# Tags of the operand tiles in the second product of a squared-ReLU MLP

## The chip, the cores and the metric

The kernel runs on one core of a Trainium2 chip. The time is that of one execution on the device in microseconds, as the median of several runs. The profile is that of one execution, and its times are counted from the start of its span. TensorE multiplies matrices (PE; PEld is its load of weights), VectorE (DVE), ScalarE (ACT) and GpSimd (POOL) work element by element, SyncE (SP) issues nearly all of the DMAs.

## The reference

A transformer block on 1024 rows of 1024 float32 values: two token mixers (latent attention and grouped attention with axial rotation), merged by gates; then the MLP that this case is about; then an embedding added through a gate, and a last norm. Only the MLP and what follows it matter here:

```python
h2 = rmsnorm(x, g_mlp[i])
u = jax.nn.relu(jnp.einsum("bsd,df->bsf", h2, w_up[i]))     # 1024 -> 4096
x = x + jnp.einsum("bsf,fd->bsd", u * u, w_down[i])         # 4096 -> 1024
h3 = rmsnorm(x, g_ple[i])
gate = jax.nn.sigmoid(jnp.einsum("bsd,de->bse", h3, w_ple_gate[i]))
x = x + gate * jnp.einsum("bsk,kd->bsd", p[i], w_ple[i])
return rmsnorm(x, g_final)
```

## The kernel before

**Products in three passes.** A float32 operand is split in two parts: the high part is its cast to float32r (on ACT), the low part is the difference of the two (on DVE, a few on POOL). A product is three matmuls: high by high, high by low, low by high (`mm3`, line 126).

**Seven block products instead of eight.** Both MLP products are made from 2 x 2 blocks by sums and differences of blocks, with seven products. The first product (`up_pair`) takes 16 pairs of column tiles, b = 0 to 15. For each it squares the four quarters after the ReLU (`uq`), forms four sums of quarters, the tiles `us` (lines 1055 to 1060; by DVE for the last pair, by POOL otherwise), and stores these and three quarters to the DRAM array `u_d` (line 1062, 256 KB each). They are the left operands of the second product. SP issues the stores in one queue with the loads.

**The second product** goes over four chunks c = 0 to 3 of 1024 of the 4096 inner values. In each chunk the block products run in the order 1, 2, 5, 6, 3, 7, 4. A block product has four steps k; in each step one left tile `da` (from `ua`, two loads of 512 KB for each block product, line 991) and one right tile `db` (from `wd`, halves of 1 MB of `w_down`, line 985, with differences `wd` minus `wd` made by POOL in `minus`, line 1198) are split by `operand`. Each is [128, 2, 512]: the high part in the first half, the low part in the second. Twelve matmuls follow in a step: three for each of four row tiles, 48 in a block product. `put` (lines 1140 and 1142) adds the finished sum to an accumulator `acc`, by copies on ACT the first time; `acc[0]` and `acc[1]` hold the residual, loaded from `x_d` (line 1084, 2 MB each). For chunk 0, the left tiles of products 1 and 2 and the first half of `wd` are loaded ahead of the last pair (`down_first`); the other loads are issued after it in the text.

**Where the operand tiles lie.** The pool `dp` has one buffer for each tag, 4 KB per partition. The tags are given in turn, `d0` to `d9`, one for each call of `operand`, in the order a, b of step 0, a, b of step 1 and so on; there are 224 calls. A tag can be written again when the matmuls that read the tile before it are done. `dp` begins at the address at which the pool `fp` of the first product began, when that pool is closed. `fp` holds, in this order, raw weights (8 KB), `p1` (8), `st` (8), `u2` (4), `u3` (4) and then five buffers `us` of 2 KB. So `d0` to `d7` cover what comes ahead of `us`, and `d8` and `d9` lie on four of the five `us` buffers. A tile that takes such a place waits until the last reader of the old one is done, for `us` the store to DRAM.

**Order.** Engines take their instructions in the order in which the scheduler wrote them; it places an instruction by priority and by its own estimate of when operands are there, so one engine's order can interleave two block products. In the text around line 1109 nothing fixes that order.

Of the kernel before, what the change touches and what calls it, by code (L numbers as in the profile page):

```python
# [10 lines left out]
F32R = mybir.dt.float32r  # L11
# [8 lines left out]
P = 128  # L20
# [33 lines left out]
def hybrid_block_kernel(ctx: ExitStack, tc, x, p, g_mix, w_in, g_qa, w_qb, g_kva, w_kvb, g_qn, g_kn,  # L54
# [34 lines left out]
    def raw_tile(name, shape):  # L89
        return wpool.tile(shape, F32, tag="raw", name=f"raw_{name}")  # L90
# [422 lines left out]
    with tc.tile_pool(name="ap", bufs=2, reuse_waits="tile") as ap:  # L513
# [273 lines left out]
        for i in range(NK + 2):  # L787
# [3 lines left out]
            d = i - 2  # L791
# [35 lines left out]
    with tc.tile_pool(name="op", bufs=2, reuse_waits="tile") as op:  # L827
# [115 lines left out]
        for n, f in enumerate((0, 2, 1)):  # L943
            t = raw_tile(f"early{f}", [P, NK, P])
# [161 lines left out]
    na, nd, np_ = [0], [0], [0]  # L1106
    with tc.tile_pool(name="dp", bufs=1, reuse_waits="tile") as dp:
        def operand(name, raw, eng):
            t = dp.tile([P, 2, 512], F32R, tag=f"d{nd[0] % 10}", name=f"d{name}")
            nd[0] += 1  # L1110
            act.copy(t[:, 0], raw)  # L1111
            eng.tensor_tensor(t[:, 1], raw, t[:, 0].bitcast(F32), ALU.subtract)  # L1112
            return t

        def product(i, c, av, bv):
# [34 lines left out]
            for k in range(4):  # L1150
                eng = pool if c == 0 and i == 1 and k < 2 else dve
                ab.append((operand(f"a{k}_{i}_{c}", av[k // 2][:, k % 2], eng), operand(f"b{k}_{i}_{c}", bv[:, k], eng)))
                if whole:
                    continue
                for s in range(4):
                    if k == 0:
                        room(s)
                    part(s, k, k + 1)
                    if k == 3:
                        put(s)  # L1160
# [205 lines left out]
```

## Time and profile before

| | |
|---|---|
| median of 3 runs | 1686.15 us (1685.62 to 1687.7) |
| profiled execution | 1688.77 us, span 1687.0 us, mean granted clock 0.972 |
| TensorE busy | 1556.5 us, 92% of the span |
| VectorE busy | 1210.6 us, 72% |
| ScalarE busy | 816.0 us, 48% |
| GpSimd busy | 729.1 us, 43% |
| DMA | 262.56 MB, mean 156 GB/s |

The span is some 2 us shorter than the execution's own time. Busy shares are means over stages with different limits: the attention up to about 700 us, the output products, the first MLP product up to 1203 us, the second from there to 1549 us, and the gate at the end.

### The profile page before, as it was taken

How to read it: one execution, taken by the hardware profiler on the slowest of the kernel's cores; microseconds unless marked ns; L12 is line 12 of the kernel's file. 1: busy time of each engine (PE TensorE's matmuls, PEld its weight loads, DVE VectorE, ACT ScalarE, POOL GpSimd, SP SyncE). 2: the span in 40 equal slices, each digit the busy share in tenths (PEclk: the TensorE clock that was granted, in tenths of full speed). 3: DMA queues.
4: the chain of work that ended last, by engine and by line, in shares of the span. 5: the costliest groups of instructions: out<-in, count | busy, mean ns of one | idle time of the engine just before them, and what ended most of it. 6: DMA issues, size and time to landing. Idle time of an engine off the chain costs nothing.

```text
span 1687.0 us, 24112 instructions
## 1 busy us (share of the span) xinstructions
PE 1556.5 (92%) x8490; PEld 1317.4 (78%) x8490; DVE 1210.6 (72%) x1967; ACT 816.0 (48%) x1583; POOL 729.1 (43%) x463
## 2 busy tenths in 40 slices
PE   7999989998989787899996999999679999998898
PEld 7998767776767565688995888888568888876898
DVE  7277227776888878655468998999556878898753
ACT  6344327776888777533354222222145444434443
POOL 4354004645777778422153422333421322253653
PEclk9999999999999999999997999999889999999999
DMA  6024558989999999945543544444936353411232
GB/s 226 26 51 114 142 150 169 209 186 197 204 176 194 197 182 201 247 153 188 175 138 112 170 150 161 139 154 153 385 103 221 101 187 113 137 63 63 88 125 77
DMA packets 437865, 262.56 MB, mean 156 GB/s; under 512 B 284520, under 2 KB 383472, under 8 KB 437360
## 3 DMA queue, kind: packets, MB, share of 16 engines
q1 hardware_dynamic: 436464, 258.92, 58.9%
q10 hardware_dynamic: 1280, 2.10, 0.6%
q8 instruction: 67, 1.10, 0.3%
q14 instruction: 54, 0.44, 0.1%
HBM read 142.41 MB, written 49.35 MB: 114 GB/s over the span
## 4 chain that ended last, share of the span: by engine, by line
PE 50%; DMA 11%; DVE 9%; ACT 7%; issue 4%; POOL 2%; SPq 1%; ACTq 0%; POOLq 0%; DVEq 0%
PE u L126 17%; PE d L126 15%; DMA PT<-hl 7%; PE wo L126 5%; PE y L126 4%; PE pg L126 3%; ACT p L594 2%; POOL hl L602 2%; PE av L772 2%; PE gt L126 1%; DVE p L591 1%; ACT hl L600 1%; DMA wd<-in_w_down_dram 1%; DVE db L1112 1%; PE pp L126 1%
## 5 line engine op out<-in xcount | busy, mean ns | idle before, releaser
L602 POOL TENSOR_TENSOR hl<-p,hl 128x1024 f16<-128x1024 f32 x128 | 279.3, 2189 | 201.0 <-PE gt L126 83.2
L126 PE MATMUL d<-db,da 128*128 128x512 f32 x1344 | 312.2, 395 | 32.8 <-ACT db L1111 25.0
L126 PEld LDWEIGHTS d<-db,da 128*128 128x128 f32 x1344 | 255.9, 191 | 88.6 <-ACT db L1111 25.4
L126 PE MATMUL u<-H_t,wop 128*128 128x512 f32 x768 | 183.3, 394 | 5.9 <-ACT H_t L900 4.6
L126 PEld LDWEIGHTS u<-H_t,wop 128*128 128x128 f32 x768 | 145.8, 190 | 38.2 <-ACT H_t L900 5.0
L591 DVE TENSOR_SCALAR_CACHE_REDUCE p<-s 128x1024 f32<-128x1024 f32 x128 | 155.6, 1218 | 16.6 <-PE s L126 6.2
L1111 ACT CAST da<-ua 128x512 fp32r<-128x512 f32 x112 | 69.7, 623 | 182.2 <-PE d L126 140.8
L594 ACT ACTIVATE p<-p,mx 128x1024 f32<-128x1024 f32 x128 | 147.2, 1150 | 9.3 <-DVE Va L458 1.5
L126 PE MATMUL u<-H_b,wop 128*128 128x512 f32 x576 | 137.8, 393 | 7.1 <-ACT wop L815 7.1
L1112 DVE TENSOR_TENSOR da<-ua,da 128x512 fp32r<-128x512 f32 x110 | 89.4, 813 | 66.7 <-ACT da L1111 66.7
L126 PEld LDWEIGHTS u<-H_b,wop 128*128 128x128 f32 x576 | 109.1, 190 | 30.2 <-ACT wop L815 7.5
L1198 POOL TENSOR_TENSOR wd<-wd,wd 128x1024 f32<-128x1024 f32 x16 | 39.3, 2458 | 203.4 <-DVE db L1112 195.8
L601 DVE TENSOR_SCALAR_CACHE_REDUCE hl<-p 128x512 f16<-128x512 f32 x128 | 87.2, 682 | 51.7 <-DMA PT<-hl 35.6
L1112 DVE TENSOR_TENSOR db<-wd,db 128x512 fp32r<-128x512 f32 x110 | 113.5, 1032 | 1.3 <-ACT db L1111 1.3
L126 PE MATMUL s<-KT,QT 96*128 96x512 f32 x384 | 102.4, 407 | 7.2 <-DVE p L591 7.1
L126 PE MATMUL gt<-hH,lo_g 128*128 128x512 f32 x256 | 102.0, 399 | 1.8 <-DVE lo_g L105 1.8
L126 PE MATMUL gt<-hH,hi_g 128*128 128x512 f32 x256 | 101.9, 398 | 1.6 <-ACT hi_g L103 1.6
L1057 POOL TENSOR_TENSOR us<-uq 128x512 f32<-128x512 f32 x15 | 19.6, 1307 | 192.6 <-DVE uq L1053 192.6
L126 PE MATMUL gt<-hL,hi_g 128*128 128x512 f32 x256 | 100.8, 394 | 0.0
L105 DVE TENSOR_TENSOR lo_g<-raw_g,hi_g 128x1024 fp32r<-128x1024 f32 x32 | 46.1, 1440 | 69.6 <-ACT hi_g L103 69.6
L600 ACT CAST hl<-p 128x512 f16<-128x512 f32 x128 | 78.7, 616 | 26.8 <-DMA PT<-hl 24.0
L126 PEld LDWEIGHTS s<-KT,QT 96*128 96x128 f32 x384 | 69.2, 191 | 24.8 <-DVE p L591 8.2
(341 smaller groups left out, 3923.3 us busy)
## 6 DMA issues: line engine op xcount, KB each, us to landing
ua<-u_d SPq DMA_DIRECT2D x56, 512.0 KB, 3.5
raw_g<-in_w_in_dram SPq DMA_DIRECT2D x32, 512.0 KB, 4.2
raw_up<-in_w_up_dram SPq DMA_DIRECT2D x32, 512.0 KB, 4.9
u_d<-us SPq DMA_DIRECT2D x64, 256.0 KB, 2.1
wd<-in_w_down_dram SPq DMA_DIRECT2D x16, 1024.0 KB, 9.4
u_d<-uq SPq DMA_DIRECT2D x48, 256.0 KB, 2.0
gates_d<-gst SPq DMA_DIRECT2D x32, 256.0 KB, 2.6
gg<-gates_d SPq DMA_DIRECT2D x16, 512.0 KB, 3.1
```

The costliest lines, as they stand in the source:

```text
L105: eng.tensor_tensor(lo, raw, hi.bitcast(F32), ALU.subtract)
L126: return [pe.matmul(ps, a, b, start=start and i == 0, stop=stop and i == len(m) - 1) for i, (a, b) in list(enumerate(m))[first:last]]
L591: dve.tensor_scalar(e, ps, 1.0, 3e38, op0=ALU.mult, op1=ALU.min, accum_out=mx)
L594: act.activation(e, e, AF.Exp, bias=mx, scale=-1.0, accum_out=sums[:, hd, qt:qt + 1])
L600: act.copy(hl[:, 0, :CUT], e[:, :CUT])
L601: dve.tensor_scalar(hl[:, 0, CUT:], e[:, CUT:], 1.0, 0.0, op0=ALU.mult, op1=ALU.max, accum_out=top)
L602: pool.tensor_tensor(hl[:, 1], e, hl[:, 0], ALU.subtract)
L772: pe.matmul(av[:, :256], values(hd, kt), PT[(2 * g + half) % 3][:, n, kt], start=(kt + n == 0), stop=(kt + n == NS))
L1057: eng.tensor_tensor(v[1], q[:, 2], q[:, 3], ALU.add)
L1111: act.copy(t[:, 0], raw)
L1112: eng.tensor_tensor(t[:, 1], raw, t[:, 0].bitcast(F32), ALU.subtract)
L1198: pool.tensor_tensor(o[:, ks], a[:, ks], b[:, ks], ALU.subtract)
```

## The change

The tag of an operand tile is computed in another way; nothing else differs. The n-th tile took tag n mod 10. Now the tiles 0 to 23 (products 1, 2 and 5 of chunk 0) take n mod 8, and those from 24 on take (n - 16) mod 10, so that tile 24 has `d8`, tile 25 `d9` and tile 26 `d0`. The pool has the same ten tags of the same size.

```diff
         def operand(name, raw, eng):
-            t = dp.tile([P, 2, 512], F32R, tag=f"d{nd[0] % 10}", name=f"d{name}")
+            n = nd[0]
             nd[0] += 1
+
+            t = dp.tile([P, 2, 512], F32R, tag=f"d{n % 8 if n < 24 else (n - 16) % 10}", name=f"d{name}")
             act.copy(t[:, 0], raw)
             eng.tensor_tensor(t[:, 1], raw, t[:, 0].bitcast(F32), ALU.subtract)
             return t
```

## Rows read from the trace of the kernel before

**Rows 1.** Page part 2: TensorE's busy tenths in 40 slices of 42.2 us.
```profile
...
PE   7999989998989787899996999999679999998898
...
```

**Rows 2.** Chain of waits, 1190 to 1260: start, duration (us), what held the chain.
```profile
...
1224.98 6.28 DMA u_d<-us
...
1231.33 0.63 ACT db L1111
...
1232.00 28.17 PE d L126 x116
```

**Rows 3.** Waits, 1190 to 1300: engine, line, waited for; total us, times, longest.
```profile
...
PE d L126 <- ACT db L1111: 25.0, 1, 25.0
ACT da L1111 <- DMA u_d<-us: 23.4, 1, 23.4
...
```

**Rows 4.** Timeline, 1185 to 1250: start, duration, what, [idle before <- releaser].
```profile
...
1203.70 3.33 PE L126 MATMUL d<-db,da 128*128 128x512 f32 x14
...
1205.27 0.62 ACT L1111 CAST db<-wd 128x512 fp32r<-128x512 f32 x1
...
1229.32 0.62 ACT L1111 CAST da<-ua 128x512 fp32r<-128x512 f32 x1 [23.43 <-DMA u_d<-us]
...
1232.00 18.20 PE L126 MATMUL d<-db,da 128*128 128x512 f32 x72 [24.96 <-ACT db L1111]
...
```

**Rows 5.** SyncE's queue in the timeline, 1165 to 1300: start and duration of issue.
```profile
...
1198.85 0.45 SPq L991 DMA_DIRECT2D ua<-u_d  x1
1200.08 0.32 SPq L1084 DMA_DIRECT2D acc<-x_d  x1
1200.67 0.37 SPq L991 DMA_DIRECT2D ua<-u_d  x1
1204.41 5.19 SPq L985 DMA_DIRECT2D wd<-in_w_down_dram  x2
1209.66 6.54 SPq L991 DMA_DIRECT2D ua<-u_d  x1
...
1217.43 0.52 SPq L991 DMA_DIRECT2D ua<-u_d  x1
1218.05 3.11 SPq L1062 DMA_DIRECT2D u_d<-us  x3
...
1224.98 0.32 SPq L1062 DMA_DIRECT2D u_d<-us  x1
1246.02 27.26 SPq L991 DMA_DIRECT2D ua<-u_d  x6
...
```

**Rows 6.** Stretches: length, busy PE, PEld, DVE, ACT, POOL (instructions), clock, DMA share, GB/s.
```profile
...
1207.00:1232.00 25.00, 0.04 (x1) 0.00 (x1) 3.36 (x7) 1.29 (x3) 9.23 (x4) 0.59 0.92 362
1232.00:1235.00 3.00, 3.00 (x7) 2.42 (x8) 1.88 (x3) 0.99 (x2) 0.00 (x0) 0.50 0.00 0
...
1240.00:1306.00 66.00, 66.00 (x293) 54.65 (x292) 46.13 (x56) 37.90 (x64) 15.36 (x6) 1.00 0.49 167
...
```

**Rows 7.** Timeline, 1185 to 1262: operand subtractions, casts, and POOL's differences.
```profile
...
1208.36 0.69 DVE L1112 TENSOR_TENSOR da<-ua,da 128x512 fp32r<-128x512 f32 x1
1208.96 0.68 DVE L1112 TENSOR_TENSOR db<-wd,db 128x512 fp32r<-128x512 f32 x1
...
1209.78 4.63 POOL L1198 TENSOR_TENSOR wd<-wd,wd 128x1024 f32<-128x1024 f32 x2 [7.60 <-issue]
...
1249.15 2.72 POOL L1198 TENSOR_TENSOR wd<-wd 128x1024 f32<-128x1024 f32 x1
1249.54 2.88 DVE L1112 TENSOR_TENSOR db<-wd,db 128x512 fp32r<-128x512 f32 x1
...
1255.22 0.62 ACT L1111 CAST da<-ua 128x512 fp32r<-128x512 f32 x1 [1.58 <-PE d L126]
1255.75 0.62 ACT L1111 CAST db<-wd 128x512 fp32r<-128x512 f32 x1
...
```

**Rows 8.** Groups by line, 1232 to 1560, TensorE: count, busy, mean ns, idle before.
```profile
...
L126 PE MATMUL d<-db,da 128*128 128x512 f32 x1330 | 308.9, 395 | 32.8 <-ACT db L1111 25.0 <-DVE db L1112 3.1 <-DVE v_ple L167 2.7
...
```

## The prediction

> **What bounds the kernel now.** The page's busy times come first: TensorE (PE) is busy 92% of the span, so the whole span can only shorten where PE stands still. The forty slices say where that is: besides the start and the end, PE falls to 6 and 7 tenths in the 29th and 30th slice (1181 to 1265 us) [rows 1]. The chain of waits of that stretch gives the story in three pieces: a store of `us` that lands at 1224.98 + 6.28 = 1231.26 us, then the cast of a `db`, then PE, which goes on at 1232.00 [rows 2]. The list of who waited for whom sizes it: PE waited 25.0 us once for that cast, and ScalarE (ACT) waited 23.4 us once, at the cast of a `da`, for the store `u_d<-us` [rows 3]. The engines' timeline shows both ends: PE runs 14 matmuls of the first product from 1203.70 to 1207.03 and then nothing for 24.96 us. ACT's eighth operand cast is at 1205.27; the ninth and the tenth come only at 1229.32 and 1231.33 [rows 4].
>
> Why a cast waits for a store: the ninth and tenth operand tiles take the tags `d8` and `d9`, which lie where the last pair's sums `us` lay, and those still have to be copied out. SyncE's queue (SP) issues the stores behind everything that it sent before: `ua`, 2 MB of `acc`, two `wd` of 1 MB, more `ua`, and then the sums, the last one at 1224.98 [rows 5]. From 1207 to 1232 the DMA engines are 92% busy at 362 GB/s [rows 6]: this is a queue that drains at its rate, and the store is at its end. Nothing that PE needs for the next products is among what is stored.
>
> The resumption comes exactly at the end of the tenth tile's cast although 34 matmuls of the first product were still to do: PE takes its instructions in their written order, and the first uses of the second product's operands stand in it after those 14.
>
> **What the change does, part by part.**
>
> *The ninth and tenth tile move from `d8`, `d9` to `d0`, `d1`.* Their first eight tags lie below the sums. That these are free of the stores, the trace shows: the eighth cast ended at 1205.89, and ACT's one long wait for a store comes right before the ninth [rows 3, 4]. What the ninth now waits for is the end of the first product's first step (12 matmuls), which read `d0` and `d1`. PE's rate in the dense stretch is 66.00 us for 293 matmuls, 0.225 us each [rows 6]; 12 of them from 1203.70 end at 1206.4. In the steady part a cast follows PE and the second one starts 0.53 us after it and takes 0.62 us [rows 7], so both are done at about 1207.6. Removed: the 24.96 us of PE's gap.
>
> *The clock.* In the gap the granted clock falls: the mean is 0.59, and it is 0.50, the lower of the two levels (1.2 of 2.4 GHz), from 1232 to 1235, where PE started 7 matmuls in 3.00 us [rows 6]. At 0.225 us they would take 1.6: 1.4 us more go with the gap.
>
> *Data for the products that come earlier.* This is what could be late next. Products run in the order 1, 2, 5, 6, 3; at 48 matmuls, 10.8 us each, they start at 1203.7, 1214.5, 1225.3, 1236.1 and 1246.9 if nothing stalls. The queue is in order and its last 256 KB land at 1231.26, so what stands behind a load gives its landing, at 362 to 400 GB/s an estimate from [rows 5, 6]. Product 5's second `ua` (issued 1198.85) has 7168 KB behind it (2048 of `acc`, 2048 of `wd`, three `ua` of 512, the four `us` of rows 5 and two `uq` at 256 each), 7.3 MB or 18 to 20 us: it lands at about 1211 to 1213, and its cast is due after 1220. Product 6's `ua` (1200.67) has 4608 KB behind it, 12 to 13 us: 1219, due 1230. Product 3's second (1217.43) has 1280 KB, 3.5 us: 1228, due 1240. The `acc` tile that product 2 adds into was sent before the first of these and is needed from about 1224. The weights' differences were formed by GpSimd (POOL) in four operations from 1209.78 on, 2.3 us each [rows 7], so both halves of `wd` had landed by then. All are in time, with 5 us and more to spare: cost nothing.
>
> *POOL and VectorE (DVE) meet.* In the old run DVE ended its last subtraction at 1209.64 and then stood still while POOL made those four in a row, 4.63 us for each two [rows 7]. Now DVE makes product 2's low halves in just that time. Where the two meet, a DVE subtraction of 0.68 us takes 2.88 and POOL's takes 2.72 [rows 7]: they take turns. The page "SBUF — State Buffer" of the Trainium skill, section "SBUF: two separate sides", has the rule: a DVE operation with two SBUF inputs and a GpSimd operation share a port pair by an exclusive lock, and the second blocks fully; the 2.88 us agree with that; it says nothing of how much of a block PE would see. By turns of 2.73 us from 1209.8, DVE ends its second to fifth subtraction at about 1213.0, 1215.7, 1218.4 and 1221.2, and the last three, 0.6 us apart, by 1223.0. PE needs the second (step 0) at 1214.5, the fourth (step 1) at 1217.4, the sixth (step 2) 2.7 us later, the eighth after that. So it waits about 1.0 us in step 1 and 0.7 us in step 2. Bounds: 0, if POOL starts later than now, and 4 x (2.88 - 0.60) = 9.1 us, if every blocked subtraction is exposed. I take 1.7, the count by turns.
>
> *PE's written order.* If product 2's first matmuls stay behind those 14, PE waits from 1206.85 to 1207.6, some 0.8 us; if the new order puts them later, nothing. I take 0.4.
>
> *Eight tags in turn instead of ten, up to the 24th tile.* An operand can be made four steps ahead instead of five. From the release by PE to the second low half a step takes about 1.15 us of casts and 1.3 us of subtractions [rows 7], 2.5 us, against three steps of 2.7 us = 8.1 us. It costs nothing as long as that holds.
>
> *The 25th and 26th tile (product 6, step 0) take `d8`, `d9` and now meet the stores.* The casts can start at 1231.3, the low halves are there at about 1234, and PE starts product 6 at 1236.1 plus the stalls above, at about 1238. Nothing, with 4 us of slack; ACT stands still a few us before, with no eviction due.
>
> *All later tiles, in ten tags as before, are shifted by a constant.* Loads and stores of the later chunks are released by the work itself and move with it. The last product holds `d0` to `d7` instead of `d6` to `d9` and `d0` to `d3`; the tiles of the last stage that lie there wait for the last matmul by either. From 1232 to 1560 PE idles 32.8 us before operand matmuls, 25.0 of them this gap [rows 8]; the other 8 lie near the end, and a shifted order may lengthen or shorten them: 0, with 2 us to either side as bounds.
>
> **Sum.** 24.96 + 1.4 - 1.7 - 0.4 = 24.3 us less. The profiled execution took 1688.77 us with a span of 1687.0; it becomes 1664.5 with a span of 1662.7. The median of the runs, 1686.15, is 2.62 us below the profiled one, so 1661.9 us is the time forecast. Without a stall it would be 26.4 us less (1659.8), with 9.1 us of blocked subtractions and 0.8 of order 16.5 less (1669.7); the 2 us of the end on both sides give 1657.8 to 1671.7.
>
> **Rivals.**
>
> 1. *The exclusive port decides.* If PE exposes each blocked subtraction, the gain is 16.5 us: 1669.7. For it: 2.88 us rows, four POOL operations in a row. Against: PE stays fully busy from 1240 to 1306 although pairs of them occur there [rows 6, 7].
> 2. *The wait moves to product 6.* Tiles 25 and 26 wait for the very same stores. From a landing at about 1236 on, each later us is lost again. For it: the stores are last in an in-order queue; against: what follows them in that queue, six loads of `ua`, was issued from 1246.02 on [rows 5]. With the stores 10 us later, six of them are lost: 1668.
> 3. *Nothing changes.* PE would stop at 1207 for something else that comes at 1231, or the low tags would wait for the stores too. Against it are the first eight casts [rows 4]: 1686.
> 4. *Slower: four steps ahead are too few.* If making a step's operands (two casts, two subtractions, each blocked) took longer than three steps of PE, 8.1 us, PE would wait in every one of the 8 steps of products 2 and 5, and from 3.1 us a step on that exceeds the 24.3 us gained. At 11.6 us for a step's operands it would be 3.5 us a step, 28 in all, and the time 1690. Against it: fully blocked they take 1.15 + 2 x 2.88 = 6.9 us, under the point at which it begins.
>
> **How the numbers follow.** The forecast has 0.78 (its own range 1658 to 1666), rival 1 0.08, rival 2 0.06, another order of the written work in the first chunk with a stall of 5 to 10 us 0.03, no change 0.03, slower 0.02. Runs of this kernel differ by some 0.1%, so about 0.2% (3.4 us) can be told from no change. Faster 0.95, same 0.03, slower 0.02. The range 1657.5 to 1671 takes in the bounds of the unknown costs and most of rivals 1 and 2.
>
> **What would show it.** Right: no wait of ACT for `u_d<-us` before the 25th operand tile, PE dense from 1203.7 on but for 1 to 2 us near 1217 to 1222, the granted clock at 1.00 from 1207 to 1240, and the last operand matmul some 24 us earlier. Rival 1: DVE rows of 2.88 us with PE waiting for `db` of DVE line 1112. Rival 2: a PE wait behind the 25th tile's cast at 1236 or later. Wrong altogether: a PE gap of over 10 us that begins between 1207 and 1250.

## The result, and the profile after

The changed kernel took 1674.38 us (median of 4 runs, 1672.75 to 1678.28), the kernel before 1686.93 us (4 runs, 1685.62 to 1688.97): a ratio of 0.9930 with an interval of 0.9911 to 0.9949. By the medians that is 12.6 us less, by the interval 8.6 to 15.0, where 24.3 were forecast. The direction was right, the size was half, and the time lies outside the range of 1657.5 to 1671.

The page shows that the dip at the start of the second product is still there. The 29th slice has 9 and the 30th 6 tenths now, of 41.8 us each:

```profile
...
PE   7999989998989888899996999999969999998898
...
```

The chain of waits of that stretch has the same head as before [rows 2]: a store of `us`, then casts, then PE. Columns: start, duration, what held the chain.

```profile
...
1218.57 4.36 DMA u_d<-us
...
1222.94 0.63 ACT da L1113
...
1224.88 0.61 DVE db L1114
...
1225.54 34.63 PE d L126 x144
```

The first row names the store that was issued last. By the program the cast waits for an earlier one, `us1` of the last pair, the first of that pair's four `us` stores in the queue.

The waits from 1190 to 1300 answer to [rows 3]. ACT waited as long as before for the store, 23.7 us against 23.4, and again at the cast of a `da`. PE waited 16.6 instead of 25.0 us:

```profile
...
ACT da L1113 <- DMA u_d<-us: 23.7, 1, 23.7
...
PE d L126 <- ACT db L1113: 16.6, 1, 16.6
...
```

The timeline answers to [rows 4]. PE now runs all 48 matmuls of the first product, to 1208.07, before it stops; before it were 14. ACT stops in the same place as before, behind the eighth cast, and goes on when the store lands:

```profile
...
1197.03 11.04 PE L126 MATMUL d<-db,da 128*128 128x512 f32 x48
...
1198.60 0.61 ACT L1113 CAST db<-wd 128x512 fp32r<-128x512 f32 x1
...
1222.94 1.14 ACT L1113 CAST da<-ua 128x512 fp32r<-128x512 f32 x2 [23.73 <-DMA u_d<-us]
...
1224.65 5.59 PE L126 MATMUL d<-db,da 128*128 128x512 f32 x13 [16.58 <-ACT db L1113]
...
```

So the wait was not removed; PE only had 34 matmuls more to do while it lasted. 25.0 - 16.6 = 8.4 us is the gain in the gap. The clock costs somewhat more than before [rows 6]: the mean of the granted clock is 0.65 in the gap and 0.68 in the 8 us after it, where PE started 22 matmuls in its 7.25 busy us. At 0.225 us each [rows 6] they would take 5.0, so 2.3 us were lost there; the prediction counted 1.4 for the kernel before. Columns as in [rows 6].

```profile
...
1207.00:1224.00 17.00, 1.07 (x5) 0.56 (x3) 0.41 (x1) 1.06 (x3) 5.72 (x3) 0.65 0.95 365
1224.00:1232.00 8.00, 7.25 (x22) 5.48 (x23) 6.48 (x11) 6.67 (x12) 0.00 (x0) 0.68 0.00 2
...
```

**How to compare such runs.** The instructions ahead of the second product are the same in both kernels, in the same order, and yet its first matmul came at 1203.7 us before and at 1197.0 after. All runs below were compared over the operand stretch instead, from the first start of a matmul `d<-db,da` to the last, which a row of each trace gives (minimum, median and maximum duration in ns, then first and last start). Before: 1549.1 - 1203.7 = 345.4 us.

```profile
...
L126 PE MATMUL d<-db,da x1344: 387/389/796, 1203.7 to 1549.1; 128*128 128x512 f32 x192
...
```

After: 1533.2 - 1197.0 = 336.2 us, 9.2 us less.

```profile
...
L126 PE MATMUL d<-db,da x1344: 387/389/796, 1197.0 to 1533.2; 128*128 128x512 f32 x192
...
```

What follows the stretch to the end of the span is 137.9 and 137.8 us. 9.2 us is therefore what the change is worth in these two traces; 6.7 of the 16.0 us between their spans came from the stages ahead, whose instructions the change leaves as they were.

**Why ACT waited again** is in the order in which its instructions were written. The program of the kernel before has, from the seventh cast on, these lines. The first number is the place in ACT's order. A name gives the left (`da`) or right (`db`) tile, the block product, the chunk, and last a running number of the program, which is not the tile's number of 0 to 223:

```
1021 L1111 CAST da_1_0_11612<-ua_11294 128x512
1022 L1111 CAST db_1_0_11615<-wd_0_11295 128x512
1023 L1111 CAST da_2_0_11634<-ua_11294 128x512
1024 L1111 CAST db_2_0_11637<-wd_0_11295 128x512
...
1041 L1111 CAST da_6_0_11796<-ua_0_0_11549 128x512
```

and the changed kernel:

```
1021 L1113 CAST da_1_0_11612<-ua_11294 128x512
1022 L1113 CAST db_1_0_11615<-wd_0_11295 128x512
1023 L1113 CAST da_6_0_11796<-ua_0_0_11549 128x512
1024 L1113 CAST da_2_0_11634<-ua_11294 128x512
1025 L1113 CAST db_2_0_11637<-wd_0_11295 128x512
```

The cast of tile 24 (the left tile of step 0 of product 6, the first to take `d8`) stands ahead of tile 8. Tiles 8 to 23 must wait for a tag that the products ahead of them still read; tile 24 has a tag that none of these uses. That the scheduler took this tag to be free by then and the data to be there, and wrote it first for that, is concluded from the order; its estimates are not on record. In the run `d8` was free only when the store had landed, and ACT went on with tile 8 only behind tile 24.

DVE's order has the same turn: tile 24's subtraction stands ahead of tile 8's. DVE waited 20.35 us behind that cast, and these are the two `da` that it then did in a row:

```profile
...
1223.59 1.29 DVE L1114 TENSOR_TENSOR da<-ua,da 128x512 fp32r<-128x512 f32 x2 [20.35 <-ACT da L1113]
...
```

### The profile page after: what moved, and what is told of

It reads as the page before. It is cut to its first block, busy times and chain, and to the rows that moved or that the text cites. A ratio compares the mean times of both kernels' runs of the same rounds, so it can differ in the third digit from the quotient of the medians.

```text
span 1671.0 us, 24113 instructions
## 1 busy us (share of the span) xinstructions
PE 1559.7 (93%) x8490; PEld 1320.2 (79%) x8490; DVE 1215.2 (73%) x1967; ACT 815.5 (49%) x1583; POOL 730.1 (44%) x463
## 4 chain that ended last, share of the span: by engine, by line
PE 48%; DMA 12%; DVE 10%; ACT 5%; issue 4%; POOL 4%; SPq 1%; POOLq 0%; ACTq 0%; DVEq 0%
PE u L126 17%; PE d L126 15%; DMA PT<-hl 7%; PE y L126 4%; PE wo L126 4%; PE pg L126 3%; POOL hl L602 2%; PE av L772 2%; PE gt L126 1%; ACT p L594 1%; ACT hl L600 1%; DMA wd<-in_w_down_dram 1%; DVE db L1114 1%; DVE p L591 1%; DMA bc<-rs_d 1%
## 5 line engine op out<-in xcount | busy, mean ns | idle before, releaser
L126 PE MATMUL d<-db,da 128*128 128x512 f32 x1344 | 312.6, 395 | 23.3 <-ACT db L1113 16.6
```

The source lines that it names most:

```text
L126: return [pe.matmul(ps, a, b, start=start and i == 0, stop=stop and i == len(m) - 1) for i, (a, b) in list(enumerate(m))[first:last]]
```

## The experiments

Theory A: ACT stands at tile 24's cast, which is written ahead of product 2's, and that makes the gap. Theory B: product 2 would have to wait until then in any case, for loads, weights or blocked subtractions. The runs take away the place in the order, the tag, or the lateness of the store, one at a time.

**The changed kernel once more.** No edit.

> The changed kernel once more, unchanged, to size what differs from run to run. From the first operand matmul of the second product to the last one it took 336.2 us, the kernel before 345.4, a gain of 9.2 us; the first matmul itself came 6.7 us earlier, in stages with the same instructions. If that head start is chance, this run has the 336 us again (335 to 338) and the wait of some 16.6 us for the cast of a db after 48 matmuls, while the first operand matmul lies anywhere from 1196 to 1205. If it belongs to the change, the first matmul is near 1197 again and the time 12 to 16 us under the kernel before.

Measured: 1673.47 us (6 runs), ratio 0.9934 (0.9915 to 0.9954), against 1684.52. The operand stretch is 1530.2 - 1194.0 = 336.2 us, PE waited 16.8 us in the gap, and the first operand matmul came at 1194.0:

```profile
...
L126 PE MATMUL d<-db,da x1344: 387/389/796, 1194.0 to 1530.2; 128*128 128x512 f32 x192
...
```

```profile
...
PE d L126 <- ACT db L1113: 16.8, 1, 16.8
...
```

The stretch repeats to 0.1 us, its start does not. This run alone does not tell whose the head start of 6.7 us was: the first matmul came even earlier than expected, and the time is 11 us under the kernel before, less than the 12 to 16 expected if the head start were the change's. Two later runs tell more. The last two below have the changed kernel's tags and one and the same order of all instructions ahead of the stretch, and begin it at 1197.9 and at 1206.1 us; so 8 us come without any difference ahead. And in the result and the six runs below with other tags than before, the median gains what the stretch gains, plus -1.0 to +3.4 us; a head start of 6.7 us in each would show there. Whether the medians' 11 to 12.6 us hold more than the 9.2 us of the stretch can't be told within their intervals.

**Eight tags for the first 56 tiles instead of 24.**

```diff
-tag=f"d{n % 8 if n < 24 else (n - 16) % 10}"
+tag=f"d{n % 8 if n < 56 else (n - 48) % 10}"
```

> The tags d0 to d7 in turn for the first 56 tiles (the whole of chunk 0) instead of 24; the first tiles on d8 and d9 belong to chunk 1. Theory A (a later tile is written ahead): whatever tile first takes d8 or d9 has a free place by the scheduler's estimate, and is written into ScalarE's order as soon as its data are thought to be there; ScalarE then waits there for the stores. So the gap stays at 16 to 20 us after 48 matmuls (d9 is free 2.5 us later than d8), operand matmuls over 335 to 340 us, time 1672 to 1679. Theory B (product 6's operands themselves were late, or those of product 2): with d8 and d9 out of chunk 0 the wait for the stores leaves it, operand matmuls over 318 to 324 us, time 1656 to 1662.

Measured: 1675.72 us, ratio 0.9944 (0.9922 to 0.9965). The operand stretch is 1533.9 - 1195.6 = 338.3 us, and the gap follows 48 matmuls again, now with a `db` at its head:

```profile
...
L126 PE MATMUL d<-db,da x1344: 387/389/796, 1195.6 to 1533.9; 128*128 128x512 f32 x192
...
```

```profile
...
ACT db L1113 <- DMA u_d<-us: 25.8, 1, 25.8
...
PE d L126 <- ACT db L1113: 18.7, 1, 18.7
...
```

ACT's order has there the cast of `db_1_1`, the right tile of step 0 of product 1 in chunk 1: tile 57, the first on `d9`, written far ahead of its number. `d9` comes free later than `d8`, hence 25.8 us instead of 23.7. So it is not product 6 that is late: in both kernels one of the two tiles that first take `d8` and `d9` is pulled to the front and waits there. The other one is not; tile 25 stood two places early in the changed kernel, and tile 56 is not among the next casts here. Theory A as expected.

**The same tags, tile 24 written behind tile 23.**

```diff
+    cast23 = []
...
-            act.copy(t[:, 0], raw)
+            cast = act.copy(t[:, 0], raw)
+            if n == 23:
+                cast23.append(cast)
+            elif n in (24, 25):
+                follow(cast, cast23[0])
```

(`follow` adds an order between two instructions and no wait.)

> The changed kernel with one more order: the casts of tiles 24 and 25 are written behind that of tile 23 in ScalarE's order; tags and waits are the same. Theory A (ScalarE stood at tile 24's cast, written ahead of product 2's): the gap after the first product goes, PE runs product 2 at once, and tile 24 meets the stores 20 us later, when they have landed or nearly so. Operand matmuls over 318 to 324 us instead of 336, time 1656 to 1662, 24 to 28 us under the kernel before. Theory B (product 2 would have to wait anyway, for blocked subtractions, loads or weights): a gap of 10 us or more between 1207 and 1230 stays and the time is 1668 or more. If the forecast's count of turns between VectorE and GpSimd is right, PE waits 1 to 2 us for a db in product 2.

Measured: 1659.32 us (1657.09 to 1662.08), ratio 0.9847 (0.9825 to 0.9868) to the kernel before. The operand stretch is 1517.8 - 1198.6 = 319.2 us:

```profile
...
L126 PE MATMUL d<-db,da x1344: 388/389/796, 1198.6 to 1517.8; 128*128 128x512 f32 x192
...
```

```profile
...
1198.63 13.99 PE L126 MATMUL d<-db,da 128*128 128x512 f32 x61
1213.64 3.02 PE L126 MATMUL d<-db,da 128*128 128x512 f32 x12 [1.02 <-DVE db L1119]
1217.04 23.19 PE L126 MATMUL d<-db,da 128*128 128x512 f32 x100 [0.38 <-DVE db L1119]
```

PE runs on through the first product into the second with 61 matmuls on record, waits 1.02 and 0.38 us for two low halves, and is dense in the rest of the view. PE has no wait here that leads to the stores; ACT stood 1.69 us at tile 25's cast, which by the program waits for the last store (the row names the load that was issued behind it), and PE did not need that tile yet. It went on 27.6 us after the first operand matmul, as tile 9 did before [rows 2, 4]:

```profile
...
1201.60 0.63 ACT L1114 CAST da<-ua 128x512 fp32r<-128x512 f32 x1 [0.78 <-issue]
...
1202.12 0.62 ACT L1114 CAST db<-wd 128x512 fp32r<-128x512 f32 x1
...
1226.18 0.62 ACT L1114 CAST db<-wd 128x512 fp32r<-128x512 f32 x1 [1.69 <-DMA ua<-u_d]
...
```

The first two rows are tiles 8 and 9. The tags, the places in memory, the queue and PE's order are those of the changed kernel; what moved is tile 24's cast in ACT's order and, with it, its subtraction in DVE's (tile 25 by two places). That was worth 336.2 - 319.2 = 17.0 us. The cast and the subtraction were not moved one without the other. Theory B is refuted: nothing else that product 2, 5 or 6 needs was late by more than the two short waits. These are the turns of DVE and POOL, which the timeline shows in this stretch:

```profile
...
1205.10 2.89 DVE L1119 TENSOR_TENSOR db<-wd,db 128x512 fp32r<-128x512 f32 x1
...
1207.91 2.88 DVE L1119 TENSOR_TENSOR da<-ua,da 128x512 fp32r<-128x512 f32 x1
...
1210.71 2.88 DVE L1119 TENSOR_TENSOR db<-wd,db 128x512 fp32r<-128x512 f32 x1
...
1213.51 2.87 DVE L1119 TENSOR_TENSOR da<-ua,da 128x512 fp32r<-128x512 f32 x1
...
1216.31 0.68 DVE L1119 TENSOR_TENSOR db<-wd,db 128x512 fp32r<-128x512 f32 x1
...
```

**Only eight tags, for all tiles.**

```diff
-tag=f"d{n % 8 if n < 24 else (n - 16) % 10}"
+tag=f"d{n % 8}"
```

> All 224 operand tiles on d0 to d7 in turn; d8 and d9 are never used, so no operand tile meets a store. Theory A: as with the order written out, operand matmuls over 318 to 326 us, time 1656 to 1664. It is above that only by what two tags fewer cost in chunks 1 to 3. The rival that eight tags are too few: PE waits in each step where VectorE and GpSimd take turns, 21 block products at 1 to 3 us, operand matmuls over 340 to 380 us and the time 1676 or more. Theory B: a gap of 10 us or more stays after the first product.

Measured: 1661.65 us, ratio 0.9861 (0.9838 to 0.9884). The operand stretch is 1522.2 - 1197.9 = 324.3 us:

```profile
...
L126 PE MATMUL d<-db,da x1344: 387/389/796, 1197.9 to 1522.2; 128*128 128x512 f32 x192
...
```

```profile
...
1197.90 13.99 PE L126 MATMUL d<-db,da 128*128 128x512 f32 x61
1212.91 3.01 PE L126 MATMUL d<-db,da 128*128 128x512 f32 x12 [1.02 <-DVE db L1114]
1216.31 250.54 PE L126 MATMUL d<-db,da 128*128 128x512 f32 x1103 [0.39 <-DVE db L1114]
1469.33 0.74 PE L126 MATMUL d<-db,da 128*128 128x512 f32 x2 [2.48 <-ACT db L1113]
...
1476.64 2.79 PE L126 MATMUL d<-db,da 128*128 128x512 f32 x11 [1.33 <-DVE db L1114]
...
1513.10 9.52 PE L126 MATMUL d<-db,da 128*128 128x512 f32 x28 [2.16 <-DVE db L1114]
...
```

With no tile on `d8` and `d9` the gap is gone as well. The stretch is 5.1 us longer than with the order written out. From 1216.31 on PE is dense for 250.54 us, through chunks 0 to 2 and into the last, so eight tags cost nothing there; the other waits are all in the last chunk, the longest 2.48 and 2.16 us. The written order of the last chunk differs too, so how much of the 5.1 us is the tags' is not shown. The rival of the prediction by which eight tags are too few costs at most that here.

**The kernel before, its stores first in the queue.** The last pair's seven stores get their place in SP's order ahead of both loads of `acc` and of the first half of `wd` for chunk 1; tags and ACT's order are those of before.

```diff
...
-    down = {}
+    down, stores = {}, []
...
-                nc.sync.dma_start(u_d[i, b], t)
+                ins = nc.sync.dma_start(u_d[i, b], t)
+                if b == NPR - 1:
+                    stores.append(ins)
...
-        nc.sync.dma_start(acc[h], x_d[h])
+        ins = nc.sync.dma_start(acc[h], x_d[h])
+        for st_ in stores:
+            follow(ins, st_)
...
-                wN = w_half(c + 1, 0)
+                wN = w_half(c + 1, 0, stores if c == 0 else ())
```

(`w_half` orders its loads behind them in the same way.)

> The kernel before with its ten tags, and in SyncE's queue the last pair's seven stores ahead of 6 MB of loads: both acc halves and the first half of the next chunk's wd. Nothing in ScalarE's order is moved. If the gap is as long as the stores take to come through that queue, then from the first operand matmul they have 3 to 4.3 MB ahead instead of 9 to 10, and land some 10 to 12.6 us after it instead of 25 to 27.6: gap of 9 to 11 us after 14 matmuls instead of 25, operand matmuls over 328 to 332 us, time 1669 to 1674. If product 1 and 2 were held by something else, or the loads moved back are now late (acc for product 2's sums), the gap stays over 20 us or a new wait of 5 us and more for acc appears.

Measured: 1672.00 us, ratio 0.9897 (0.9872 to 0.9921). The operand stretch is 1533.4 - 1203.5 = 329.9 us, and the gap 10.39 us:

```profile
...
L126 PE MATMUL d<-db,da x1344: 387/389/796, 1203.5 to 1533.4; 128*128 128x512 f32 x192
...
```

```profile
...
1203.51 3.33 PE L126 MATMUL d<-db,da 128*128 128x512 f32 x14
1217.24 15.07 PE L126 MATMUL d<-db,da 128*128 128x512 f32 x56 [10.39 <-ACT db L1117]
```

The gap follows the store through the queue: with 6 MB less ahead it is 14.6 us shorter. At the 362 GB/s of [rows 6] those loads would take 17 us, an estimate. No wait for `acc` of 5 us or more came in its place.

**The changed kernel, its stores first in the queue.** The same move, on the changed kernel; ACT's order keeps tile 24 in front.

> The changed kernel with the same move of the seven stores in SyncE's queue; tile 24's cast still stands ahead of product 2's in ScalarE's order. Theory A (ScalarE stands there for the store): the store lands about 10 us after the first operand matmul, just when the 48 matmuls end, so the gap shrinks from 16.7 to 1 to 3 us and operand matmuls take 320 to 324 us, time 1658 to 1664. If the place in the order did harm by itself, whatever the store's time, the gap stays above 8 us and the time above 1667.

Measured: 1663.72 us, ratio 0.9861 (0.9844 to 0.9877). The operand stretch is 1522.9 - 1197.9 = 325.0 us, 1 us over the range expected:

```profile
...
L126 PE MATMUL d<-db,da x1344: 388/389/792, 1197.9 to 1522.9; 128*128 128x512 f32 x192
...
```

```profile
...
1197.94 11.04 PE L126 MATMUL d<-db,da 128*128 128x512 f32 x48
1209.87 0.50 PE L126 MATMUL d<-db,da 128*128 128x512 f32 x1 [0.89 <-ACT db L1119]
1215.06 17.20 PE L126 MATMUL d<-db,da 128*128 128x512 f32 x66 [4.69 <-DVE db L1120]
```

The wait for the cast shrank from 16.6 to 0.89 us, as theory A has it. What was not expected is the second wait, 4.69 us for the low half of a `db`. The timeline shows its cause: the casts came together at 1208.16, in the middle of POOL's four differences, and the first two subtractions took 5.59 us in turns with them. One of these two is tile 24's, which no product needs yet.

```profile
...
1208.16 1.14 ACT L1119 CAST da<-ua 128x512 fp32r<-128x512 f32 x2 [8.03 <-DMA u_d<-us]
1208.74 5.12 POOL L1206 TENSOR_TENSOR wd<-wd 128x1024 f32<-128x1024 f32 x2
1208.82 5.59 DVE L1120 TENSOR_TENSOR da<-ua,da 128x512 fp32r<-128x512 f32 x2 [4.92 <-ACT da L1119]
...
```

**Both: the order written out and the stores first.**

> The changed kernel with tile 24's cast behind tile 23's, and the stores ahead in the queue as well. With the order right no engine waited for a store, so an earlier store buys nothing: operand matmuls over 318 to 321 us, time 1657 to 1662, the same as with the order alone. If the loads moved back are late for product 2's sums it is 2 to 6 us above that; if the store still held ScalarE somewhere, below it.

Measured: 1660.72 us (1655.92 to 1665.01), ratio 0.9844 (0.9823 to 0.9865). The operand stretch is 1525.3 - 1206.1 = 319.2 us, the same as with the order alone:

```profile
...
L126 PE MATMUL d<-db,da x1344: 387/389/793, 1206.1 to 1525.3; 128*128 128x512 f32 x192
...
```

With the order right PE stands behind no store, and an earlier store buys nothing. Set beside the run before it, which differs only in the order, this one also says what the place in the order still costs when the stores come first: 325.0 - 319.2 = 5.8 us. The order alone is the version to keep: it beats the kernel before by 1.5% and the changed one by 17.0 us of the stretch.

## Why the prediction was wrong

*The place of the gap and its cause* were right: PE stood for a cast that stood for a store at the end of an in-order queue. The move of the stores, which shortened the gap from 25.0 to 10.4 us with every other engine's order as before, shows it. The reading of the slices left something out: PE also falls to 6 tenths in the 22nd, and to 7 in the 14th and 16th [rows 1]. The change touches none of these.

*Tiles 8 and 9 on `d0` and `d1`* could not do in the changed kernel what was said of them, since they stood behind tile 24 until 1222.9. With the order written out they did: their casts ended 4.1 us after the first operand matmul, where 1207.6 - 1203.7 = 3.9 were forecast.

*The gain of 9.2 us* came by another way than the forecast's. The wait stayed (23.7 us of ACT, 23.4 before). PE's new written order put product 2's first matmuls behind all 48 of product 1, so that PE had 34 more to do while it lasted. The prediction had that order only as a cost of 0 to 0.8 us; that the direction came out right owes something to luck.

*The step that failed* is the one on the 25th and 26th tile: "The casts can start at 1231.3, the low halves are there at about 1234, and PE starts product 6 at 1236.1 plus the stalls above, at about 1238. Nothing, with 4 us of slack". It reckoned when the tile is needed and when its place is free, and took it that its cast stands in ACT's order where its number puts it. ACT's order is written by the scheduler, and in the changed kernel it has tile 24 ahead of tiles 8 to 23. The runs put 17.0 us in place of that "nothing", and a PE gap of 16.6 us that begins at 1208.1, which the prediction had named as the sign that it is wrong altogether. Among its chances it had 0.03 for another written order in the first chunk, with a stall of 5 to 10 us; that is the kind of thing that came, but it was not worked out and was put too small. The prediction did look at the written order, but at PE's alone (0.4 us), where the old trace showed an instruction out of turn; the same could be asked of ACT, whose instructions take tags. The second rival had the right wait at the wrong place, behind product 5, where by its count it costs nothing up to a landing at 1236.

*The rest of the sum* can be checked on the run with the order written out, which is the kernel that the prediction had in mind. It shortens the stretch by 345.4 - 319.2 = 26.2 us, where 24.3 were summed. The turns of DVE and POOL were counted at 1.0 + 0.7 = 1.7 us and cost 1.02 + 0.38 = 1.4. PE's order was put at 0.4 and cost nothing: product 2's first matmuls left their place behind the first 14. Most of the rest lies near the end of the stretch, where PE waited 7.9 us before and 6.3 in this run; the prediction took 0 there, with 2 us to either side. The loads and weights were in time, and eight tags up to the 24th tile cost nothing. The median of that kernel is 1659.32 us, the forecast 1661.9.

*The exclusive port* as a rival decided nothing in the changed kernel, where DVE stood still while POOL worked. In the run of the changed kernel with the stores first it took back most of 4.7 us. The page "SBUF — State Buffer" of the Trainium skill, section "SBUF: two separate sides", says that the one that comes second is blocked fully. The traces agree, with subtractions of 2.88 us in the run with the order written out and 5.59 us for two in that with the stores first, against 0.68 us alone.

## What to carry to other kernels

When a buffer is given to another tile, look not only at who waits for it but at where that tile's first instruction then stands in its engine's order: a scheduler that places by its own estimate can pull a far later tile to the front, and an engine that takes its instructions in order then holds everything behind it, here 16 casts for 23.7 us. The trap was a place that comes free only with a store's landing. Where a late consumer has to take such a place, write its order out; that was worth 17.0 us here, the change itself 9.2.

## What the runs showed that was not expected

The time up to the second product differs by up to 12 us between the traces of this case (first operand matmul at 1194.0 to 1206.1 us), and by 8 us between two with the same instructions ahead; the cause is open. The operand stretch of the changed kernel was 336.2 us in both of its traces, and that with the order written out 319.2 with either order of the queue. A difference of 1% in this kernel is better read from the stretch that the edit touches, since the medians carry the rest as noise. In the gap of 16.6 us the granted clock fell as it did in that of 25.0 (mean 0.59 [rows 6]): a mean of 0.65 in the 17 us up to 1224, and 0.68 in the 8 us in which PE was already at work again.
